# A Fourier front with a root for each of its first two tiles, even and odd sums in one PSUM bank, and two input loads on another queue

## The chip, the cores and the metric

The kernel runs on one core of a Trainium2 chip. Its time is that of one execution on the device, in microseconds (us), as the median of several runs. The engines are TensorE (PE: matmuls; PEld: its weight loads), VectorE (DVE), ScalarE (ACT) and GpSimd (POOL); SyncE (SP) issues most transfers, GpSimd the accumulating ones and a few more.

## The reference

Two sequences of 512 tokens with 1024 features pass through two layers. Layer 0 mixes by a Fourier transform, layer 1 by grouped attention, and each is followed by a squared-ReLU MLP; a last norm ends it. All data are float32. The change touches only the mixer of layer 0:

```python
def rms_norm(x, g):
    x32 = x.astype(jnp.float32)
    y = x32 * lax.rsqrt(jnp.mean(x32 * x32, axis=-1, keepdims=True) + EPS)
    return (y * g.astype(jnp.float32)).astype(x.dtype)

def fourier_mix(h, w_out):
    B, S, _ = h.shape
    hg = h.astype(jnp.float32).reshape(B, S, N_FGROUPS, F_GROUP)
    f = jnp.fft.fft2(hg, axes=(1, 3), norm="ortho").real
    f = f.reshape(B, S, D_MODEL).astype(h.dtype)
    return f @ w_out
...
    x = x + fourier_mix(rms_norm(x, fourier_norm[j]), fourier_w_out[j])
```

The real part of the transform over tokens and the 128 features of a group is a product of cosines minus a product of sines. The kernel folds both axes: sums and differences of mirrored features (`p`, plus, and `m`, minus), and even and odd parts over tokens, halve the work.

## The kernel before, in words

The front runs from the start to about 72 us, in an order written out by hand for all engines (`manual_schedule`): each engine works through its own list strictly in the order in which the program names the operations, and waits where an operand, a buffer or a bank isn't ready.

The two sequences are handled one after the other. **The first** (`q == 0`) is done "exactly", with float32 operands on TensorE, where each product is two instructions; everything later splits its operands into a high and a low float32r half and multiplies three times (`mm3`, lines 80 to 83).

*The operands of the first sequence.* Four tiles of 128 tokens come in (`begin`, line 322). `Front` (from line 365) takes two tiles each: `f0` the first two, `f1` the others. Per tile: the sum of squares (ScalarE, L124), the gain (VectorE, L379), the minus (L392) and the plus (L383). `chain` runs the six steps of a reciprocal root (L135 to L140: one on ScalarE, five on VectorE) for both tiles of a `Front` at once. `scale_both` (L409, ScalarE) scales the plus, eight Nyquist columns and the minus of one tile of `f0`; that gives the first and the second operand, `parts[0]` and `parts[1]`. `f1` scales its first tile (L403) and adds or subtracts its second (`combine`, L417 to L419, VectorE) into the third operand, `parts[2]`.

*The token transform.* Features lie in four blocks of 128 (`j`). For each block `exact_even` (L473) sums three operands times cosines in one PSUM bank and `exact_odd` (L476) three operands times sines in another; `exact_nyq` (L479) is one more row set, which ScalarE and VectorE copy into `an` (L565, L566). There are eight banks, so `transform` takes blocks 0 to 2 first, operand by operand, evacuates each with two ScalarE copies (L496, L497), runs the feature stage of block 0, then block 3 and the rest. `idle` (L545) gives TensorE 61 products without use until the data are there.

*The feature stage.* `feat_stage` makes `u` (L508, L513), `v` (L521) and a Nyquist row set `en` (L522) of each block; `split` (L86 on ScalarE, then L87 on VectorE) writes their high and low halves. `nyq_out` (L535, L536) does so for `en`.

*The output weights.* `Fold` loads two halves of a block's weights on SP (L318, L319). `minus` subtracts them on VectorE (L614) and adds them by a GpSimd transfer (L615); `odd` splits the difference (L86, L87); `even_hi` and `even_lo` split the sum (L624, L628). `FoldNyq.load` prepares the Nyquist weights, a write and three reads through DRAM on GpSimd's queue (L646, L648). `odd_outs` multiplies all four blocks into eight output banks (96 matmuls in L81 to L83), which `odd_put` evacuates on ScalarE (L689, L690). `even_outs` then does the eight even outputs one by one, 13 matmuls each, the last in L666; each needs a bank that an `odd_put` has freed. `even_put` adds them on VectorE (L695).

*The second sequence.* Its tiles are loaded on SP (L299) and prepared by `g0` and `g1` between the steps above: squares, gain, minus, an adding transfer for the plus (`plus_there`, L388, GpSimd), the root, the scaling (L403), `combine` (L431 to L434, VectorE) and the splits (L443, L448). Then `transform(1)` runs, with the same code as for the first but split operands.

What decides the order of the work is thus the written lists, the eight banks, SP's and GpSimd's queues in order, and the slots of the pools.

Of the kernel before, what the change touches and what calls it, by code (L numbers as in the profile page):

```python
# [19 lines left out]
P = 128  # L20
D = 1024
# [23 lines left out]
def trunk_kernel(ctx, tc, x_in, xt_in, y_out, tables, rope, gfour, gcol, grow, gfin,  # L45
# [319 lines left out]
    class Front:  # L365


        def __init__(self, q, c):
            self.q, self.c = q, c
            self.ss, self.r = small(2), small(2)  # L370
            self.steps = rsqrt_steps(self.r[:, :2], self.ss[:, :2], 2, 1.0 / D)
            self.xg, self.p, self.m = [None] * 2, [None] * 2, [None] * 2

# [31 lines left out]
        def scale_both(self, i):  # L405
            if i == 0:
                self.n = sm.tile([P, 2, 5, 8], F32, tag="ny", name=nm("ny"), bufs=2, padded_shape=[P, 2, 8, 8])
            for out, x in ((self.p[i], self.p[i]), (self.n[:, i], eights(self.m[i])), (self.m[i], self.m[i])):
                nc.scalar.activation(out, x, AF.Copy, scale=self.r[:, i : i + 1])  # L409
            parts.append((self.p[i], self.m[i], self.n[:, i]))  # L410

        def combine(self):
            (p1, p2), (m1, m2), r, w = self.p, self.m, self.r, 8
            stt = nc.vector.scalar_tensor_tensor
            if self.q == 0:
                n = sm.tile([P, 5, 8], F32, tag="ny", name=nm("ny"), bufs=2, padded_shape=[P, 16, 8])
                stt(n, eights(m2), r[:, 1:2], eights(m1), ALU.mult, ALU.add)  # L417
                stt(m2, m2, r[:, 1:2], m1, ALU.mult, ALU.subtract)
                stt(p1, p2, r[:, 1:2], p1, ALU.mult, ALU.add)  # L419
                parts.append((p1, m2, n))  # L420
                return
# [49 lines left out]

    def exact_even(k, j, o):
        nc.tensor.matmul(o[:, :258], parts[k][0][:, j * P : (j + 1) * P], cosX[k], start=k == 0, stop=k == 2)  # L473

    def exact_odd(k, j, v):
        nc.tensor.matmul(v[:, :256], parts[k][1][:, j * P : (j + 1) * P], sinX[k], start=k == 0, stop=k == 2)  # L476
# [15 lines left out]

    def seq_evac(q, o, v):
        if q == 0:
            t = slot([P, 514], F32)
            nc.scalar.copy(t[:, :258], o[:, :258])  # L496
            nc.scalar.copy(t[:, 258:], v[:, :256])  # L497
            return t[:, :258], t[:, 258:]
# [12 lines left out]
    def feat_stage(q, j, a, b, an, en, u=None):  # L511
        if q == 0:
            nc.tensor.matmul(u[:, :258], ftX[:, :P], a, start=False, stop=True)  # L513
# [6 lines left out]
        if q == 0:  # L520
            nc.tensor.matmul(v[:, :256], ftX[:, P:], b, start=True, stop=True)  # L521
            nc.tensor.matmul(en[0:72, :258], pickX[:, pick], a, start=j == 0, stop=j == 3)  # L522
# [10 lines left out]
    def nyq_out(q, en):  # L533
        t = slot([P, 258], F32R)[0:72]
        nc.scalar.copy(t, en[0:72, :258])  # L535
        nc.vector.tensor_sub(t[64:72], en[64:72, :258], f32(t[64:72]))  # L536
        un[q] = t
# [9 lines left out]
    def transform(q, mid=lambda: None, hook=lambda at, j: None):  # L547
        on, ov = ps(), [(ps(), ps()) for _ in range(3)]
        if q == 0:
            for k in range(2):  # L550
                for j in range(3):
                    exact_even(k, j, ov[j][0])
                exact_nyq(k, on)
                for j in range(3):
                    exact_odd(k, j, ov[j][1])
            mid()
            exact_nyq(2, on)
        else:
            seq_nyq(q, 0, on)
            for j in range(3):  # L560
                seq_part(q, j, 0, *ov[j])
            mid()
            seq_nyq(q, 1, on)
        en = ps()
        nc.scalar.copy(an[0:40], on[0:40, :258])  # L565
        nc.vector.tensor_sub(an[32:40], on[32:40, :258], f32(an[32:40]))  # L566
        ab = []
        for j in range(3):
            if q == 0:
                exact_odd(2, j, ov[j][1])  # L570
                exact_even(2, j, ov[j][0])
            else:
                seq_part(q, j, 1, *ov[j])
            ab.append(seq_evac(q, *ov[j]))
            hook("seq", j)
        us = [None] * 4
        if q == 0:
            us[0] = feat_nyq(ps(), 0, True)
        feat_stage(q, 0, *ab[0], an, en, us[0])
        hook("feat", 0)  # L580
        o3 = ps(), ps()
        if q == 0:
            for k in range(3):
                exact_even(k, 3, o3[0])
            for k in range(3):
                exact_odd(k, 3, o3[1])
        else:
            for c in range(2):
                seq_part(q, 3, c, *o3)
        ab.append(seq_evac(q, *o3))  # L590
        hook("seq", 3)
        if q == 0:
            us[1:] = [feat_nyq(ps(), j, True) for j in range(1, 4)]
        feat_stage(q, 1, *ab[1], an, en, us[1])
        hook("feat", 1)
        feat_stage(q, 2, *ab[2], an, en, us[2])
        hook("feat", 2)
        feat_stage(q, 3, *ab[3], an, en, us[3])
# [32 lines left out]
    class FoldNyq:  # L631
# [7 lines left out]
        def load(self):  # L639
# [6 lines left out]
            nc.gpsimd.dma_start(self.d.rearrange("i a (b f) -> (a b) i f", b=16), f32(h[:, :2]))  # L646
            for r, i in ((0, 0), (32, 1), (64, 0)):
# [54 lines left out]
    with tc.manual_schedule(engines={ET.PE, ET.Activation, ET.DVE, ET.Pool, ET.SP}):  # L702
# [16 lines left out]
        f1.squares(0)  # L719
        f0.minus(1)  # L720
        f0.plus(1)
        f0.scale_both(0)
        f1.gain(0)
        f1.squares(1)
        f1.chain(1, 2)
        f0.scale_both(1)
        f1.minus(0)
# [1321 lines left out]
```

## Time and profile before

| what | value |
|---|---|
| three timed runs | 1680.16, 1681.12, 1679.12 us; median 1680.16 |
| the profiled execution | 1682.5 us |
| its span, first to last instruction | 1680.5 us |
| mean granted TensorE clock | 0.998 |
| ScalarE, GpSimd busy | 873.4 us (52%), 394.5 us (23%) |
| transfers | 302.99 MB, mean 180 GB/s |

A line of a timeline reads: start, duration (both us), engine, line of the program, operation, what is written from what (with buffer numbers left out), shape and type, how many alike were merged; in brackets the time for which the engine stood still before it and what ended that. A line of a table of groups has the count, then busy time and mean ns of one, then the idle time ahead. A line of the table of waits says who waited for whom: total us, times, longest. In a row of the table of stretches each engine's busy time is followed by the number of its instructions that touch the stretch, then come the granted clock, the share of the DMA engines' time and GB/s.

### The profile page before, as it was taken

The numbers are of one execution on the slowest core, as the hardware profiler recorded it, in microseconds if no ns is written. First come the engines' busy times: TensorE is split into PE (matmuls) and PEld (weight loads), VectorE is DVE, ScalarE is ACT, GpSimd is POOL, SyncE is SP. The second block draws the span as 40 slices with busy tenths as digits, with TensorE's granted clock in tenths as the row PEclk, the third lists the DMA queues.
The fourth block names the chain that finished last, engine by engine and source line by source line (L and its number), as shares of the span: only waits on it lengthen the run. The fifth ranks groups of instructions, "written<-read, shape, count | busy, mean of one in ns | idle before, by whom it ended". The sixth has DMA issues, their size and how long they took to land.

```text
span 1680.5 us, 22279 instructions
## 1 busy us (share of the span) xinstructions
PE 1666.0 (99%) x7845; PEld 1387.7 (83%) x7845; DVE 1258.9 (75%) x1848; ACT 873.4 (52%) x1537; POOL 394.5 (23%) x364
## 2 busy tenths in 40 slices
PE   9999999999999999999999999999999999999998
PEld 8988888888888888788878888888888888888887
DVE  8879776557786779869888877777855487878865
ACT  6766444456343425447698854554544553433334
POOL 3321443221000001325544303004422220000002
PEclk9999999999999999999999999999999999999999
DMA  9843655459775757425501146334544696757532
GB/s 310 262 151 111 209 194 182 145 176 371 242 231 170 254 171 225 168 65 196 168 1 39 63 164 224 124 114 160 209 156 155 226 367 203 232 158 237 176 102 100
DMA packets 122047, 302.99 MB, mean 180 GB/s; under 512 B 12200, under 2 KB 13352, under 8 KB 121936
## 3 DMA queue, kind: packets, MB, share of 16 engines
q1 hardware_dynamic: 98576, 254.05, 43.6%
q0 software_dynamic: 8960, 21.05, 5.9%
q10 hardware_dynamic: 14400, 26.48, 4.2%
q8 instruction: 61, 1.00, 0.2%
q14 instruction: 50, 0.41, 0.1%
HBM read 218.11 MB, written 82.38 MB: 179 GB/s over the span
## 4 chain that ended last, share of the span: by engine, by line
PE 87%; DVE 6%; ACT 3%; issue 2%; DMA 2%; POOL 0%; SPq 0%; DVEq 0%; ACTq 0%; POOLq 0%
PE ps L907 69%; PE ps L83 5%; PE ps L81 5%; PE ps L82 5%; PE ps L1482 1%; DVE w L87 1%; ACT t L1474 1%; ACT u L86 1%; DVE u L87 1%; DVE u L219 1%; DVE u L235 1%; DVE u L1113 0%; DMA u<-w_four 0%; DMA u<-x 0%; PE ps L172 0%
## 5 line engine op out<-in xcount | busy, mean ns | idle before, releaser
L907 PE MATMUL ps<-u,w 128*128 128x512 f32 x4944 | 1133.3, 390 | 2.9 <-DVE w L87 2.1
L907 PEld LDWEIGHTS ps<-u,w 128*128 128x128 f32 x4944 | 927.5, 188 | 199.1 <-DVE w L87 3.2
L86 ACT CAST w<-raw 128x1024 fp32r<-128x1024 f32 (+1 forms) x216 | 214.0, 996 | 310.9 <-PE ps L907 229.0
L87 DVE TENSOR_TENSOR w<-raw,w 128x1024 fp32r<-128x1024 f32 (+1 forms) x216 | 252.3, 1172 | 77.6 <-ACT w L86 77.3
L86 ACT CAST u<-u 128x1024 fp32r<-128x1024 f32 x144 | 145.2, 1049 | 83.8 <-PE ps L907 36.5
L87 DVE TENSOR_TENSOR u<-u,u 128x1024 fp32r<-128x1024 f32 x144 | 173.3, 1230 | 19.0 <-ACT u L86 17.9
L907 PE MATMUL ps<-u,u 128*128 128x512 f32 x600 | 143.1, 389 | 0.1
L1142 POOL DMA_DIRECT2D raw<-w_sum x32 | 27.7, 866 | 469.3 <-DMA raw<-w_sum 197.9
L1113 DVE TENSOR_TENSOR u<-ps,u 128x512 f32<-128x512 f32 x160 | 109.6, 686 | 37.2 <-PE ps L907 34.4
L1023 POOL TENSOR_TENSOR u<-u 128x512 f32<-128x512 f32 x28 | 37.7, 1345 | 424.7 <-ACT u L920 424.7
L907 PEld LDWEIGHTS ps<-u,u 128*128 128x128 f32 x600 | 112.5, 188 | 23.8 <-ACT u L938 0.5
L81 PE MATMUL ps<-u,u 128*128 128x512 f32 (+2 forms) x340 | 128.8, 381 | 0.4 <-ACT t L1474 0.3
L82 PE MATMUL ps<-u,u 128*128 128x512 f32 (+2 forms) x340 | 124.2, 366 | 0.4 <-DVE u L87 0.3
L83 PE MATMUL ps<-u,u 128*128 128x512 f32 (+2 forms) x340 | 124.4, 366 | 0.1
L164 POOL TENSOR_TENSOR t<-t,t 128x512 f32<-128x512 f32 (+1 forms) x54 | 77.8, 1446 | 190.6 <-ACT t L160 189.9
L919 ACT ACTIVATE t<-t 128x512 f32<-128x512 f32 x64 | 40.5, 632 | 109.8 <-DVE t L992 99.8
L87 DVE TENSOR_TENSOR u<-ps,u 128x512 fp32r<-128x512 f32 (+3 forms) x112 | 68.5, 635 | 7.9 <-ACT u L86 7.3
L83 PEld LDWEIGHTS ps<-u,u 128*128 128x128 f32 x340 | 64.2, 189 | 10.5 <-DVE u L448 0.5
L81 PEld LDWEIGHTS ps<-u,u 128*128 128x128 f32 x340 | 64.3, 189 | 10.1 <-ACT u L86 1.5
L82 PEld LDWEIGHTS ps<-u,u 128*128 128x128 f32 x340 | 64.4, 189 | 9.2 <-DVE u L87 1.4
L979 DVE TENSOR_TENSOR t<-ps,u 128x512 f32<-128x512 f32 x32 | 22.0, 688 | 60.5 <-PE ps L907 52.7
L1476 POOL TENSOR_SCALAR t<-t,s 128x512 f32<-128x512 f32 x64 | 47.3, 740 | 74.0 <-DVE s L1475 60.1
(260 smaller groups left out, 2029.7 us busy)
## 6 DMA issues: line engine op xcount, KB each, us to landing
raw<-w_up SPq DMA_DIRECT2D x80, 512.0 KB, 4.6
u<-spill_t SPq DMA_DIRECT2D x60, 512.0 KB, 6.8
raw<-w_sum SPq DMA_DIRECT2D x56, 512.0 KB, 5.7
u<-spill_b SPq DMA_DIRECT2D x45, 512.0 KB, 6.2
spill_t<-u SPq DMA_DIRECT2D x84, 256.0 KB, 2.0
spill_b<-t ACTq DMA_DIRECT2D x60, 256.0 KB, 4.3
raw<-w_row SPq DMA_DIRECT2D x28, 512.0 KB, 5.2
park<-u SPq DMA_DIRECT2D x24, 512.0 KB, 4.5
```

The costliest lines, as they stand in the source:

```text
L81: nc.tensor.matmul(out, lh, rh, start=first, stop=False)
L82: nc.tensor.matmul(out, lh, rl, start=False, stop=False)
L83: nc.tensor.matmul(out, ll, rh, start=False, stop=last)
L86: nc.scalar.copy(dst_hi, src)
L87: eng.tensor_sub(dst_lo, src, f32(dst_hi))
L164: nc.gpsimd.tensor_add(acc[q][:, :n], acc[q][:, :n], s[:, :n])
L907: nc.tensor.matmul(o, w[x][:, sl], h[k][y], start=first and k + i == 0, stop=k == n - 1 and i == 2, skip_group_check=not first)
L919: nc.scalar.activation(t, src, AF.Relu)
L1023: eng.tensor_sub(t[:, 0], b12, b11)
L1113: nc.vector.tensor_add(x, o, x)
L1142: nc.gpsimd.dma_start(s[:, 1], w[:, 3], accum_op=ALU.add)
L1476: nc.gpsimd.tensor_scalar(p, p, sm_[:, :1], 1.0, ALU.mult, ALU.mult)
```

## The change

For the first sequence only:

- `f0` takes a root for each of its two tiles (`alone`), plus ahead of minus; `scale_both` is cut into `scale_plus` and `scale_minus`.
- `combine` for `f1` is cut into `combine_minus` and `combine_plus`; the odd part of the third operand comes first.
- Even and odd sums of a block share one bank: columns 0 to 256 and 257 to 511. `exact_open` writes zeros (the Nyquist buffer, then still zero, as moving operand) over the whole bank with `start`, and all other products add. The four blocks so take four banks, and all four go through operands 1 and 2 ahead of operand 3; of operand 3 come the odd sums, the Nyquist rows, the even sums. One ScalarE copy of 512 columns evacuates a block (`exact_evac`). The feature stages of all four follow, with 257 and 255 columns where there were 258 and 256.
- The warm-up has 46 products where it had 61.
- `fold[0].odd` and `fold[1].minus` come after the four evacuations, `fold[2].minus` after the feature stage of block 0, `fold[1].odd` after that of block 1, `fold[3].minus`, `fold[2].odd` and `fold[3].odd` after that of block 3. The reads of the Nyquist weights (`get`) come behind two weight additions on GpSimd's queue.
- The work of `g0` that stood ahead of the odd outputs' code is spread between the even weights' splits; its root's last four steps come after the third low part, and its first scaling stands ahead of all eight `odd_put` on ScalarE, of which four now come ahead of its second.
- Tiles 2 and 3 of the second sequence are loaded on GpSimd's queue, behind the last weight addition.

```diff
+        def alone(self, i, a, b):
+            if i not in self.each:
+                c = slice(i, i + 1)
+                self.each[i] = rsqrt_steps(self.r[:, c], self.ss[:, c], 1, 1.0 / D)
+            for step in self.each[i][a:b]:
+                step()
...
+    def exact_open(o):
+        nc.tensor.matmul(o, an[:, :P], filler.unsqueeze(1).broadcast_to([P, 4, P]), start=True, stop=True)
+
     def exact_even(k, j, o):
-        nc.tensor.matmul(o[:, :258], parts[k][0][:, j * P : (j + 1) * P], cosX[k], start=k == 0, stop=k == 2)
-
-    def exact_odd(k, j, v):
-        nc.tensor.matmul(v[:, :256], parts[k][1][:, j * P : (j + 1) * P], sinX[k], start=k == 0, stop=k == 2)
+        nc.tensor.matmul(o[:, :257], parts[k][0][:, j * P : (j + 1) * P], cosX[k][:, :257], start=False, stop=k == 2,
+                         skip_group_check=True)
+
+    def exact_odd(k, j, o):
+        nc.tensor.matmul(o[:, 257:], parts[k][1][:, j * P : (j + 1) * P], sinX[k][:, 1:256], start=False, stop=k == 2,
+                         skip_group_check=True)
...
+    def exact_evac(o):
+        t = slot([P, 512], F32)
+        nc.scalar.copy(t, o)
+        return t[:, :257], t[:, 257:]
...
+    def transform_exact(o, mid, hook):
+        on = ps()
+        for k in range(2):
+            for j in range(4):
+                exact_even(k, j, o[j])
+            exact_nyq(k, on)
+            for j in range(4):
+                exact_odd(k, j, o[j])
+        mid()
+        for j in range(4):
+            exact_odd(2, j, o[j])
+        exact_nyq(2, on)
+        put_an(on)
+        ab = []
+        for j in range(4):
+            exact_even(2, j, o[j])
+            ab.append(exact_evac(o[j]))
+        hook("seq", 3)
+        en = ps()
+        us = [feat_nyq(ps(), j, True) for j in range(4)]
+        for j in range(4):
+            feat_stage(0, j, *ab[j], an, en, us[j])
+            if j < 3:
+                hook("feat", j)
+        nyq_out(0, en)
+        hook("feat", 3)
...
-        idle(ps(), 61)
+        idle(ps(), 46)
+        pairs = [ps() for _ in range(4)]
+        for o in pairs:
+            exact_open(o)
         f0.squares(0)
         f0.gain(0)
+        f0.plus(0)
+        f0.alone(0, 0, 2)
+        f0.squares(1)
+        f0.alone(0, 2, 6)
         f0.minus(0)
-        f0.plus(0)
-        f0.squares(1)
+        f0.scale_plus(0)
         f0.gain(1)
-        f0.chain(0, 6)
+        f0.alone(1, 0, 2)
+        f0.scale_minus(0)
+        f0.alone(1, 2, 6)
         f1.squares(0)
...
         def hook0(at, j):
             if at == "seq":
...
+                fold[1].minus()
+                wn.get()
+                fold[0].odd()
+            elif j == 0:
+                fold[2].minus()
+            elif j == 1:
+                fold[1].odd()
             elif j == 3:
+                fold[3].minus()
+                for t in range(2, 4):
+                    load_x(1, t, nc.gpsimd)
+                fold[2].odd()
                 fold[3].odd()
...
         o = odd_outs(0, range(KC))
+        fold[0].even_hi()
+        g0.squares(0)
+        fold[0].even_lo()
+        g0.gain(0)
+        fold[1].even_hi()
+        g0.minus(0)
+        g0.plus_there(0)
+        g0.squares(1)
         g0.chain(0, 2)
-        fold[0].even_hi()
-        fold[1].even_hi()
+        fold[1].even_lo()
+        fold[2].even_hi()
+        g0.gain(1)
+        fold[3].even_hi()
+        g0.minus(1)
+        g0.plus_there(1)
+        fold[2].even_lo()
         g0.chain(2, 6)
-        fold[0].even_lo()
-        fold[1].even_lo()
+        fold[3].even_lo()
         g0.scale(slice(0, 1))
-        fold[2].even_hi()
-        fold[2].even_lo()
-        odd_put(0, 0, o[0])
-        fold[3].even_hi()
-        fold[3].even_lo()
-        for fo in range(1, 4):
+        for fo in range(4):
             odd_put(0, fo, o[fo])
         g0.scale(slice(1, 2))
```

Behind the front the instructions of every engine follow in the same order as before.

More of the change, by code (lines that the diff above doesn't have):

```diff
@@ L512, in feat_stage @@
         if q == 0:
-            nc.tensor.matmul(u[:, :258], ftX[:, :P], a, start=False, stop=True)
+            nc.tensor.matmul(u[:, :257], ftX[:, :P], a, start=False, stop=True)
         else:
@@ L545, in idle, with put_an @@
             nc.tensor.matmul(o[:, :256], filler, filler.unsqueeze(1).broadcast_to([P, 2, P]), start=True, stop=True)
[L547 to L564, printed above, removed]
+    def put_an(on):
@@ L567, in transform @@
+    def transform(q, hook):
+        on, ov = ps(), [(ps(), ps()) for _ in range(3)]
+        seq_nyq(q, 0, on)
+        for j in range(3):
+            seq_part(q, j, 0, *ov[j])
+        seq_nyq(q, 1, on)
+        en = ps()
+        put_an(on)
         ab = []
         for j in range(3):
[L569 to L573, printed above, removed]
+            seq_part(q, j, 1, *ov[j])
@@ L840, in hook1 @@
                     square(0, 7)
-        transform(1, hook=hook1)
+        transform(1, hook1)
         for fo in range(KC):
```

118 lines of the change are left out of this document (47 added, 71 removed).

## The prediction

> **What bounds the kernel now.** I read the page first (engines and chain), then TensorE's waits, then the timeline of the first 60 us, the only stretch whose instructions the change touches. The profiled execution took 1682.5 us for a span of 1680.5 us, so 2.0 us lie around the span; the median of the three timed runs is 1680.16, that is 2.3 us under the profiled one. I work against 1682.5 and shift at the end.
>
> ```profile
> span 1680.5 us, 22279 instructions
> ...
> PE 1666.0 (99%) x7845; PEld 1387.7 (83%) x7845; DVE 1258.9 (75%) x1848; ACT 873.4 (52%) x1537; POOL 394.5 (23%) x364
> ...
> PE 87%; DVE 6%; ACT 3%; issue 2%; DMA 2%; POOL 0%; SPq 0%; DVEq 0%; ACTq 0%; POOLq 0%
> ```
>
> ```profile
> PE ps L907 <- DVE w L87: 2.1, 2, 1.9
> ...
> PE ps L473 <- ACT t L409: 1.0, 1, 1.0
> ...
> PE ps L83 <- DVE w L628: 0.5, 1, 0.5
> ```
>
> TensorE is 99% busy and holds 87% of the chain that ended last. Its whole execution has few waits, and two of the three longest lie in the front: 1.0 us before the first Fourier product (L473) and 0.5 us in the first even output (L83). From there on the engine has next to no slack, so I let a shift of the front pass to the end one for one. What the change can save is a microsecond or two at the start; what it can cost is the cover under which VectorE and ScalarE prepare the next stage. So the sum is made over three in-order engines.
>
> **The start.** The rows of the first tile, before:
>
> ```profile
> 6.08 1.23 DVE L379 TENSOR_TENSOR u<-u,u 128x1024 f32<-128x1024 f32 x1 [4.97 <-DMA u<-x]
> 7.34 0.69 DVE L392 TENSOR_TENSOR t<-u 128x512 f32<-128x512 f32 x1
> ...
> 9.69 0.16 DVE L135 TENSOR_SCALAR s<-s 128x2 f32<-128x2 f32 x1
> ...
> 10.34 0.16 DVE L140 SCALAR_TENSOR_TENSOR s<-s,s 128x2 f32<-128x2 f32 x1
> ...
> 10.59 0.71 ACT L409 ACTIVATE t<-t,s 128x512 f32<-128x512 f32 x1
> ...
> 11.35 1.57 PE L473 MATMUL ps<-u,t 128*128 128x258 f32 x6 [1.03 <-ACT t L409]
> ```
>
> The root over two tiles stands behind the second tile's gain. After: gain at 6.08, plus at 7.34 (0.61 until the next), then the tile's own root, 9.69 to 10.50, 0.81 us for five steps, ends at 8.76; ScalarE follows 0.09 later, 0.71 long, and TensorE starts at 9.6: **-1.75 us**. The shortened warm-up and the four opening products have no row before. Bounds: 15 warm-up products fewer free 15 x 0.15 = 2.25 us (61 took 9.16 us), four openings of 128x512 cost nothing at best and 4 x 0.39 = 1.6 us at worst (mean of the costliest matmul group, 390 ns). The warm-up so ends before 10.0; I take no cost, and 0.4 at worst is swallowed by the wait for the third operand.
>
> **TensorE up to the feature stage.**
>
> ```profile
> 12.85 0.63 PE L479 MATMUL ps<-u,ny 128*40 128x258 f32 x2
> ...
> 13.41 1.56 PE L476 MATMUL ps<-u,t 128*128 128x256 f32 x6
> ...
> 22.96 1.47 PE L473 MATMUL ps<-u,t 128*128 128x258 f32 x6
> ...
> 24.26 1.46 PE L476 MATMUL ps<-u,t 128*128 128x256 f32 x6
> ...
> 29.64 0.47 PE L81 MATMUL ps<-u,u 128*128 128x256 f32 x1
> ```
>
> Six of these instructions take 24.26 - 22.96 = 1.30 us, 0.217 each (a product is two of them); a Nyquist pair 0.56 (12.85 to 13.41). The columns lost (258 to 257, 256 to 255) are under 0.5%: nothing. Four blocks and two operands are 2 x (16 x 0.217 + 0.56) = 8.1, with 0.1 to 0.2 at each switch 8.5: TensorE wants the third operand at 18.1. VectorE gives its odd part at about 18.5, whose last two steps now are
>
> ```profile
> 17.32 0.30 DVE L417 SCALAR_TENSOR_TENSOR ny<-t,s,t 128x40 f32<-128x40 f32 x1
> ...
> 17.66 0.75 DVE L418 SCALAR_TENSOR_TENSOR t<-t,s,t 128x512 f32<-128x512 f32 x1
> ```
>
> From 8.76 on: minus 0.61, gain 1.14, second root 0.81, plus and minus 1.22, two gains 2.28, third root 0.81, two minuses and a plus 1.83, Nyquist rows 0.3, combination 0.75. Then odd 1.73, Nyquist 0.56, even 1.73, four products with the Nyquist rows 0.7, twelve feature pairs of 0.434: the feature stage ends at 28.4 where the odd outputs now begin at 29.64. A lead of **1.2 us** is left there.
>
> **What the lead meets: VectorE.** Before, ScalarE copied block 0 and went straight on to the weight split. Now the split of `fold[0]` stands behind the copies of all four blocks. The rows for its price:
>
> ```profile
> L86 ACT CAST u<-u 128x1024 fp32r<-128x1024 f32 x4 | 4.3, 1064 | 0.0
> ...
> L181 ACT COPY t<-ps 128x512 f32<-128x512 f32 x2 | 1.2, 582 | 0.0
> ```
>
> ```profile
> 20.69 1.23 DVE L614 TENSOR_TENSOR u<-raw,u 128x1024 f32<-128x1024 f32 x1
> ...
> 21.83 1.22 DVE L87 TENSOR_TENSOR u<-u,u 128x1024 fp32r<-128x1024 f32 x1
> ...
> 28.29 2.12 DVE L87 TENSOR_TENSOR u<-ps,u 128x257 fp32r<-128x257 f32 x6
> ```
>
> Block 0 is whole at 18.5 + 1.73 + 0.56 + 0.43 + 0.15 = 21.4; four copies at 0.55 reach 23.6, the cast 24.65, and VectorE subtracts at 24.75. It has begun `fold[0].minus` at 19.7, behind the plus sums of the third operand, has `fold[1].minus` done by 22.7 and then stands still for some **2.0 us**; before, L87 followed L614 at 21.83 without a gap. From 24.75 VectorE has no more gaps, and its order is fixed: nine 1024-wide operations (six for the odd weights and the minuses left, three even low parts) at 1.14, two gains at 1.25, two minuses at 0.61, eight PSUM differences at 0.35 (L87, six in 2.12), the Nyquist difference 0.4 and the root of `g0` 0.8: 10.3 + 2.5 + 1.2 + 2.8 + 0.4 + 0.8 = 18.0. The root of `g0` is ready at **42.8**.
>
> **The wait that decides.**
>
> ```profile
> 36.96 0.16 DVE L140 SCALAR_TENSOR_TENSOR s<-s,s 128x2 f32<-128x2 f32 x1
> 37.04 2.36 DVE L628 TENSOR_TENSOR w<-raw,w 128x1024 fp32r<-128x1024 f32 x2
> ...
> 42.05 1.22 DVE L628 TENSOR_TENSOR w<-u,w 128x1024 fp32r<-128x1024 f32 x1 [1.26 <-ACT w L624]
> ```
>
> ```profile
> 37.16 0.73 ACT L403 ACTIVATE t<-t,s 128x512 f32<-128x512 f32 x1
> ...
> 39.44 0.36 ACT L689 COPY u<-ps 128x255 f32<-128x255 f32 x1
> 39.70 0.39 ACT L690 ACTIVATE u<-ps 128x255 f32<-128x255 f32 x1
> ...
> 43.51 0.76 ACT L403 ACTIVATE u<-u,s 128x512 f32<-128x512 f32 x1
> ```
>
> ```profile
> 41.34 0.28 PE L81 MATMUL ps<-u,w 128*128 128x258 f32 x1
> 41.46 0.29 PE L82 MATMUL ps<-u,w 128*128 128x258 f32 x1
> ...
> 43.33 0.39 PE L83 MATMUL ps<-u,w 128*128 128x258 f32 x1 [0.50 <-DVE w L628]
> ```
>
> Two L628 in 2.36 us of 1.22 each give the 1.14. The even outputs' matmuls start 0.12 apart (41.34, 41.46), and the odd outputs' are as long. Before, the root (36.96) came ahead of the even low parts, and ScalarE's scaling (37.16) and first evacuation (39.44) were done before TensorE asked for a bank at 41.34. After, three low parts stand ahead of the root, and on ScalarE all eight evacuations stand behind the scaling that waits for it. The odd outputs fill all eight banks, so the first even output can't begin before `odd_put(0)`: 42.8 + 0.1 + 0.62 + 0.5 = 44.0. Before it began at 41.34 and lost 0.5, in effect 41.84: **+2.2 us**, in which the lead of 1.2 is gone. The second scaling falls at 42.9 + 0.62 + 4 x 0.52 = 45.6 against 43.51, **+2.1**, and with it what prepares the second sequence. As the transfer of the last even weights bound its low part (42.05) and no longer does, I round down: both engines arrive **2.0 us** later at the second transform, where little slack is left to swallow it:
>
> ```profile
> 58.38 0.68 DVE L448 TENSOR_TENSOR u<-t,u 128x512 fp32r<-128x512 f32 x1
> ```
>
> ```profile
> 59.12 0.38 PE L83 MATMUL ps<-u,u 128*128 128x256 f32 x1
> ```
>
> TensorE's product at 59.12 follows the end of this difference (59.06) at once. Profiled 1682.5 + 2.0 = 1684.5; for the median 1680.16 + 2.0 = **1682.2 us**.
>
> **The moved loads.** Two input tiles leave SP's queue for GpSimd's, behind the four weight additions and ahead of the two additions of `g0`. Earlier bytes become later ones, so nothing is won or lost by volume. The issues on GpSimd:
>
> ```profile
> L388 POOL DMA_DIRECT2D u<-u x4: 854/866/893, 36.3 to 51.5; - x4
> ...
> DMA to landing us min/median/max: 3.3/4.4/6.0
> ```
>
> After, the second addition of `g0` can't be issued before VectorE's minus at about 41.0 and lands between 44.3 and 47.0; the combination wants it at 46.4. I take the median, no cost; up to 0.6 if late.
>
> **Rivals.**
>
> *A: the idle gap slows TensorE's clock.* The odd outputs start at 28.4, lose 0.5 to banks freed by VectorE, take 96 x 0.12 and end near 40.4; until 44.0 the engine waits 3.6 us. The kernel's own start shows what a rested engine does:
>
> ```profile
> 2.00:3.00 1.00, 1.00 (x6) 1.00 (x6) 0.00 (x0) 0.65 (x2) 0.45 (x1) 1.00 0.87 180
> ...
> 5.00:6.00 1.00, 1.00 (x11) 1.00 (x10) 0.00 (x0) 0.00 (x0) 0.00 (x0) 1.00 1.07 434
> ```
>
> Six warm-up products touch a microsecond at first, eleven after about 4 us, at a granted clock of 1.00 in both. If 3.6 us of rest bring that back, some 4 us run at about half speed, 1.7 us more: 1683.9. [...] No row before shows a gap of that length. Chance 0.15.
>
> *B: the lead survives (the other side).* If VectorE keeps pace, because ScalarE's four copies overlap the products more than I count and its 1024-wide rows run closer, so that the root of `g0` is there by 39.5, the evacuations finish before TensorE asks at 40.1: the 1.2 us stay, with the 0.5 of L83. The price is -1.7: 1678.5. For it stand the shorter start and the 1.3 us in which VectorE waited for the last weight's transfer at 42.05. Against it stand 18.0 us of fixed VectorE work behind 24.75. Chance 0.12.
>
> *C: the additions behind the moved loads come late.* If they land at 47 or more, the second sequence's operands are late by another 1 us: 1683.2. Chance 0.12. That the first root wins nothing at all, because something else starts TensorE at 11.35, changes little: VectorE decides either way, and it is inside the forecast.
>
> **How the numbers follow.** Forecast 0.61 at 1682.2 (1681.0 to 1683.4); A 0.15, B 0.12, C 0.12. 1679.0 to 1684.8 leaves out a third of B, the late half of A with C on top, and ends of the others: under 0.2. A measurement of this kernel tells about 0.2% from no change, 3.4 us: 1676.8 to 1683.5. Faster than that only B at its best, 0.04; slower two thirds of A, a third of C and the forecast's upper end, 0.24; within, 0.72.
>
> **What would show it.** Right: first L492 product at 9.6, odd outputs from about 28.4, a VectorE gap of 2 us before the first 1024-wide L87 near 24.7, the root of `g0` near 43, a TensorE wait of 3 to 4 us before the first even output, evacuated by ScalarE. Wrong: that wait missing or put down to a DMA; an even output's matmuls at twice their 0.12 us (A); the combination of `g0` waiting for a DMA (C); a shift at 58 us that isn't found at the end.

## The result and the profile after

The changed kernel takes 1684.50 us (median of 10 runs, 1682.22 to 1686.53), the kernel before 1679.47 us beside it (10 runs, 1678.22 to 1684.17): a ratio of **1.0025, 95% interval 1.0015 to 1.0034**, or some +4.2 us (the quotient of the two medians, 1.0030, lies in that interval). Forecast were +2.0, and 1681.0 to 1683.4 as the band around them; the whole range was 1679.0 to 1684.8, and 1684.50 lies at its upper end. The profiled execution after took 1684.58 us, its span 1682.7 us.

From the page of the kernel after (span, engines, chain by engine):

```profile
span 1682.7 us, 22264 instructions
...
PE 1666.0 (99%) x7834; PEld 1388.0 (82%) x7834; DVE 1259.0 (75%) x1853; ACT 873.2 (52%) x1535; POOL 393.8 (23%) x366
...
PE 85%; DVE 6%; ACT 3%; DMA 2%; issue 2%; POOL 0%; DVEq 0%; ACTq 0%; POOLq 0%; SPq 0%
```

TensorE's sum hasn't moved by 0.1 us, so the page doesn't find the loss. TensorE's waits do:

```profile
PE ps L81 <- ACT u L719: 4.0, 1, 4.0
...
PE ps L945 <- DVE w L87: 0.8, 2, 0.6
```

The first row is new: the first even output waits for the first evacuation of an odd one. VectorE, then ScalarE, on the way there:

```profile
21.30 0.42 DVE L573 TENSOR_TENSOR u<-ps,u 8x258 fp32r<-8x258 f32 x1 [0.51 <-ACT u L572]
21.75 1.23 DVE L641 TENSOR_TENSOR u<-raw,u 128x1024 f32<-128x1024 f32 x1
24.50 1.23 DVE L87 TENSOR_TENSOR u<-u,u 128x1024 fp32r<-128x1024 f32 x1 [1.52 <-ACT u L86]
...
42.99 0.16 DVE L140 SCALAR_TENSOR_TENSOR s<-s,s 128x2 f32<-128x2 f32 x1
...
46.73 0.75 DVE L449 SCALAR_TENSOR_TENSOR u<-u,s,u 128x512 f32<-128x512 f32 x1 [1.02 <-ACT u L412]
```

```profile
43.19 0.72 ACT L412 ACTIVATE t<-t,s 128x512 f32<-128x512 f32 x1 [3.42 <-DVE s L140]
43.81 0.35 ACT L718 COPY u<-ps 128x255 f32<-128x255 f32 x1
44.07 0.38 ACT L719 ACTIVATE u<-ps 128x255 f32<-128x255 f32 x1
...
45.91 0.78 ACT L412 ACTIVATE u<-u,s 128x512 f32<-128x512 f32 x1
```

The split of `fold[0]` stands behind the four copies (1.52 us of rest), the root of `g0` comes at 42.99, the scaling that ScalarE waits 3.42 us for is the first of its list, and the first bank is free at about 44.5. So far this is the chain that was forecast. The new thing is TensorE behind the wait:

```profile
9.50 1.68 PE L492 MATMUL ps<-u,t 128*128 128x257 f32 x7
...
44.50 0.58 PE L81 MATMUL ps<-u,w 128*128 128x258 f32 x1 [3.98 <-ACT u L719]
44.88 0.42 PE L82 MATMUL ps<-u,w 128*128 128x258 f32 x1
45.10 0.42 PE L83 MATMUL ps<-u,w 128*128 128x258 f32 x1
...
49.61 0.31 PE L82 MATMUL ps<-u,w 128*128 128x258 f32 x1
49.76 0.28 PE L83 MATMUL ps<-u,w 128*128 128x258 f32 x1
49.88 0.28 PE L695 MATMUL ps<-u,u 72*128 72x258 f32 x1
```

From 44.88 to 49.61 the matmuls start 0.215 us apart; at 49.76 they are back to the 0.12 of the kernel before. These are 22 intervals of 0.095 us too much, **2.1 us**. The table of stretches shows the cause as the granted clock (third number from the end of a row):

```profile
41.00:42.00 1.00, 0.00 (x0) 0.00 (x0) 1.00 (x2) 0.00 (x0) 0.02 (x1) 1.00 0.77 129
42.00:43.00 1.00, 0.00 (x0) 0.00 (x0) 0.90 (x5) 0.00 (x0) 0.86 (x1) 0.91 0.02 4
43.00:44.00 1.00, 0.00 (x0) 0.00 (x0) 1.00 (x2) 0.81 (x2) 0.76 (x1) 0.50 0.65 115
...
48.00:49.00 1.00, 1.00 (x7) 1.00 (x7) 0.84 (x3) 1.00 (x5) 0.00 (x0) 0.50 1.01 319
49.00:50.00 1.00, 1.00 (x8) 1.00 (x7) 0.47 (x1) 0.97 (x2) 0.74 (x1) 0.68 1.18 385
50.00:51.00 1.00, 1.00 (x11) 1.00 (x10) 1.00 (x2) 1.00 (x2) 0.16 (x1) 1.00 0.60 141
```

A mean of 0.91 between 1.00 and 0.50 puts the fall at 42.82, in the middle of the rest; 0.68 puts the return at 49.64. The page's row of 40 slices doesn't show 6.8 us, and the means of the two profiled executions (0.997 against 0.998) hardly do, since the kernel before has a slow phase of its own in that execution (at 697.7 us, shown further down). Over many runs the mean does tell: the kernel after stands at 0.996 to 0.998 in all ten, the kernel before, as run beside the experiments, at 0.999 in 80 of 102. Single values say little: the last microseconds of both profiled executions stand at 0.50 too (1677.3 to 1680.5 before, 1677.8 to 1682.7 after), so that without such a phase the mean would be an estimated 0.999; the two counts together point to a fall in most executions of the kernel after.

To compare executions I count from the first gain on VectorE, since the first tile lands at another time in each (that gain starts between 5.67 and 6.94 us). Each column is the start of an instruction in the timeline of the profiled execution, less that gain's start: the first Fourier product, the first odd output, the last step of `g0`'s root, the first even output, the second transform's first matmul (shape 128*40), and the first L172 product, with which the front ends. The ratio is against the kernel before on the same chip.

| kernel | product | odd | root | even(0) | 2nd transform | front ends | ratio (95%) |
|---|---|---|---|---|---|---|---|
| before | 5.27 | 23.56 | 30.88 | 35.26 | 48.60 | 65.87 | 1 |
| after | 3.72 | 22.29 | 37.21 | 38.72 | 53.58 | 70.19 | 1.0025 (1.0015 to 1.0034) |
| keep_busy | 3.47 | 22.29 | 37.22 | 38.73 | 51.35 | 68.74 | 1.0018 (1.0010 to 1.0026) |
| evac_first | 3.49 | 22.31 | 37.25 | 34.61 | 51.45 | 68.06 | 1.0017 (1.0008 to 1.0025) |
| split_early | 3.48 | 22.30 | 36.25 | 37.76 | 53.07 | 69.68 | 1.0020 (1.0011 to 1.0029) |
| loads_back | 3.49 | 22.29 | 37.24 | 38.75 | 53.91 | 70.54 | 1.0026 (1.0016 to 1.0036) |
| root_alone | 3.48 | 24.12 | 31.44 | 35.81 | 48.31 | 65.08 | 1.0007 (0.9998 to 1.0015) |
| root_before_low | 3.70 | 22.29 | 34.33 | 35.85 | 50.43 | 67.04 | 1.0011 (1.0003 to 1.0020) |
| split_evac_first | 3.56 | 22.30 | 36.25 | 33.99 | 48.96 | 65.60 | 0.9999 (0.9991 to 1.0008) |
| split_evac_gpsimd | 3.93 | 22.29 | 36.04 | 34.30 | 48.77 | 65.38 | 0.9999 (0.9990 to 1.0007) |
| low_first | 3.48 | 22.29 | 38.77 | 34.00 | 47.85 | 71.31 | 1.0020 (1.0011 to 1.0029) |
| before_low_first | 5.25 | 23.54 | 40.92 | 36.16 | 49.97 | 71.07 | 1.0032 (1.0020 to 1.0045) |
| low_between | 3.48 | 22.31 | 37.40 | 34.00 | 46.49 | 68.71 | 1.0024 (1.0015 to 1.0033) |
| odd_sums_first | 3.48 | 22.28 | 37.38 | 33.98 | 48.37 | 69.06 | 1.0024 (1.0015 to 1.0033) |

The front of the kernel after ends 4.32 us later, and the whole is 4.2 us longer: the shift passes to the end. Per row the two agree within some 2 us, so the landmarks say where time goes and the ratios how much of it is certain.

### The profile page after: what moved, and what is told of

The parts are those of the page before. It is cut to its first block, busy times and chain, and to the rows that moved or that the text cites. A ratio compares the mean times of both kernels' runs of the same rounds, so it can differ in the third digit from the quotient of the medians.

```text
span 1682.7 us, 22264 instructions
## 1 busy us (share of the span) xinstructions
PE 1666.0 (99%) x7834; PEld 1388.0 (82%) x7834; DVE 1259.0 (75%) x1853; ACT 873.2 (52%) x1535; POOL 393.8 (23%) x366
## 4 chain that ended last, share of the span: by engine, by line
PE 85%; DVE 6%; ACT 3%; DMA 2%; issue 2%; POOL 0%; DVEq 0%; ACTq 0%; POOLq 0%; SPq 0%
PE ps L945 67%; PE ps L81 5%; PE ps L82 5%; PE ps L83 5%; DMA raw<-w_sum 1%; PE ps L1520 1%; ACT u L86 1%; ACT t L1512 1%; DVE w L87 1%; DVE u L87 1%; DVE u L219 1%; DMA u<-w_qkv 1%; DVE u L1151 1%; DVE u L235 1%; PE ps L172 0%
## 5 line engine op out<-in xcount | busy, mean ns | idle before, releaser
L87 DVE TENSOR_TENSOR u<-ps,u 128x512 fp32r<-128x512 f32 (+3 forms) x112 | 68.5, 635 | 8.0 <-ACT u L86 7.5
```

The lines of the kernel that those rows point to most:

```text
L87: eng.tensor_sub(dst_lo, src, f32(dst_hi))
```

## The experiments

The theory after the result: the loss is the late first bank (the forecast's chain) and the slow clock that the rest brings on (rival A on top). Rivals: the moved loads, the new form of the transform itself, or VectorE's list alone. Line numbers are those of each kernel.

**keep_busy** fills the rest: TensorE does the last odd output twice more, 24 matmuls that write the same sums again.

```diff
         o = odd_outs(0, range(KC))
+        for _ in range(2):
+            for k in range(4):
+                u, fs = uv[0, k][:, :, 256:512], slice(7 * P, 8 * P)
+                mm3(o[7], wo[k][0][:, fs], wo[k][1][:, fs], u[:, 0], u[:, 1], k == 0, k == 3)
```

> The changed kernel, but TensorE sums the last odd output two more times after the first (24 matmuls, 2.9 us, the same numbers again); the wait for the bank stays, only its rest is filled. Theory: the rest before the first even output shrinks from 4.0 to about 1.1 us while that output begins at the same 44.5; its matmuls are 0.12 us apart instead of 0.215, so the clock's share is measured by itself: 22 matmuls x 0.095 = 2.1 us less than the changed kernel, ratio to the kernel before about 1.0012. Rival (VectorE bounds the stretch from 50 to 60 us anyway, so a slow clock costs nothing): time as of the changed kernel, ratio 1.0025, even with matmuls 0.12 apart. Rival (the half speed has another cause than the rest, such as the evacuations or transfers at that place): matmuls still 0.215 apart.

The even output starts as late as in the kernel after (38.73), after a rest of 1.1 us, and its matmuls are 0.122 apart, so the half speed came from the rest. In the stretches:

```profile
45.00:46.00 1.00, 0.33 (x2) 0.33 (x3) 1.00 (x2) 1.00 (x5) 1.00 (x3) 1.00 1.02 176
46.00:47.00 1.00, 1.00 (x11) 1.00 (x10) 0.89 (x3) 1.00 (x5) 1.00 (x3) 1.00 0.35 25
```

Eleven matmuls in a microsecond at a clock of 1.00. The second transform starts 2.23 us earlier than in the kernel after, the price of the clock; 0.8 of it goes again before the front ends, where TensorE now waits 0.3 us for VectorE's last split. What is left at the end of the front, +2.87 us, is the price of the late bank without the clock. The ratio alone doesn't settle this: 1.0018 (1.0012 was expected) is not told from 1.0025, so the split into 2.87 and 1.45 rests on the landmarks of one execution each. The mean clock agrees: 0.999 in seven of twelve runs, never reached by the kernel after.

**evac_first** puts ScalarE's first four evacuations ahead of the scaling that waits for the root.

```diff
-        g0.scale(slice(0, 1))
         for fo in range(4):
             odd_put(0, fo, o[fo])
+        g0.scale(slice(0, 1))
         g0.scale(slice(1, 2))
```

> The changed kernel with the first four evacuations of the odd outputs moved ahead of the first scaling of g0 on ScalarE; nothing else differs. Theory (the evacuations stand behind a scaling that waits for VectorE's late root, TensorE so rests 4.0 us and comes back at half speed): the first even output begins near 40.5 us; TensorE then waits in it for the second, third and fourth low part in pieces of at most 2 us, until VectorE has written the fourth near 44.3; matmuls stay 0.12 us apart. The even outputs end near 57 instead of 59.3, and the kernel takes about 3 to 4 us less than the changed one: ratio to the kernel before 1.0000 to 1.0008. Rival (VectorE's list is late whatever ScalarE does, the wait on ScalarE only shows it): no more than 1 us is won, ratio 1.0020 or above. Rival (moved loads): ratio as of the changed kernel, 1.0025.

The even output starts 4.11 us earlier and the front ends only 2.13 earlier. Two waits for the low parts take the place of the one removed, and the stretches show what they do:

```profile
PE ps L83 <- DVE w L655: 2.1, 2, 1.2
```

```profile
44.00:45.00 1.00, 0.04 (x1) 0.00 (x0) 1.00 (x2) 0.94 (x2) 0.89 (x1) 1.00 0.80 141
45.00:46.00 1.00, 0.78 (x5) 0.78 (x6) 1.00 (x2) 1.00 (x4) 1.00 (x4) 0.95 0.71 121
46.00:47.00 1.00, 1.00 (x7) 1.00 (x6) 1.00 (x4) 0.81 (x4) 1.00 (x3) 0.50 0.48 53
```

Two rests of 0.97 and 1.18 us, 0.6 us of matmuls between them, are followed by the half clock as well, from 45.9 to 49.3. The expectation had the matmuls 0.12 us apart and a ratio of at most 1.0008; the wait for the bank was the cause of the late start, as it said, but the clock takes part of the gain.

**split_early** takes `fold[0].odd` and `fold[1].minus` behind the first of the four copies.

```diff
             ab.append(exact_evac(o[j]))
-        hook("seq", 3)
+            hook("seq", j)
...
```

> The changed kernel with the second weight subtraction and the first odd weight split put behind the first block's evacuation instead of the fourth's. Theory: VectorE's gap of 1.5 us before its first 1024-wide split closes, all that follows on it up to the root of g0 comes 1.0 to 1.5 us earlier (root near 41.8 instead of 43.1), TensorE's rest falls to 2.5 to 3 us. If a rest of that length doesn't bring the slow clock back, the kernel takes 3 to 3.5 us less than the changed one (ratio 1.0004 to 1.0008); if it does, 1.0 to 1.5 us less (ratio about 1.0017). Rival (evacuations of the other blocks now come late and TensorE loses what VectorE wins): the feature stage ends 0.5 us or more later and the time stays at 1.0025.

VectorE's rest falls from 1.52 to 0.5 us, and the root comes 0.96 us earlier. The wait shrinks only by 0.37 to 3.6, since the odd outputs, without their wait of 0.35 us for a bank, end 0.6 earlier too, and the half clock stays (0.216 apart). The forecast's gap was a real term, worth 1 us at the root and 0.5 at the end of the front.

**loads_back** puts the two moved loads back on SP's queue.

```diff
-        for t in range(2):
+        for t in range(NT):
             load_x(1, t)
...
-                for t in range(2, 4):
-                    load_x(1, t, nc.gpsimd)
```

> The changed kernel with the two input tiles of the second sequence back on SP's queue. Theory: nothing that decides hangs on them; ratio to the kernel before as of the changed kernel, 1.0025, within 0.0005, and the root of g0 still near 43. Rival C (the additions behind the moved loads come late): about 1 us less, and the combination of g0 earlier by that.

Every landmark is that of the kernel after to 0.35 us. The moved loads cost nothing, as the combination's wait for ScalarE instead of a transfer (46.73 above) already said.

**root_alone** gives the kernel before the root per tile, plus ahead of minus, and 54 warm-up products; its transform is as it was.

```diff
-        idle(ps(), 61)
+        idle(ps(), 54)
         f0.squares(0)
         f0.gain(0)
-        f0.minus(0)
         f0.plus(0)
+        f0.alone(0, 0, 2)
         f0.squares(1)
+        f0.alone(0, 2, 6)
...
```

> The kernel before with one part of the change alone: a root for each of the two first tiles, plus ahead of minus, 54 fillers. Theory (the early start is real but nothing behind it uses it, because the third operand and then VectorE's fixed work set the pace): first product 3.5 to 3.7 us after the first gain instead of 5.3, odd outputs within 0.3 us of 23.6, root of g0 within 0.3 us of 30.9, ratio 1.0000 (0.9995 to 1.0005). Rival (the early start is worth its length): odd outputs at 21.8, ratio 0.9990. Rival (the rest that opens in front of the third operand slows TensorE): a clock of 0.5 behind it and a ratio over 1.0005.

The first product comes 1.79 us earlier and the odd outputs 0.56 later: what is won at the start is spent in one wait for the third operand.

```profile
PE ps L491 <- DVE ny L429: 1.8, 1, 1.8
```

The expectation had the odd outputs and the root within 0.3 us of the kernel before; both come some 0.55 late, and the front ends 0.79 earlier all the same, which stays unexplained. Behind that wait the products keep their pace (pairs start 0.43 us apart, at 20.40, 20.83 and 21.26, or 0.217 an instruction as in the kernel before), so the last rival falls. The early start by itself buys nothing that the ratio shows (1.0007, not told from 1). So the lead of 1.27 us in the kernel after comes with the changed transform; that it has more to do ahead of that operand is my reading, not tried by itself.

**root_before_low** has `g0`'s gains and root ahead of the four low parts. (What this and later expectations call odd sums are `g0`'s minus and plus.)

```diff
-        fold[0].even_lo()
         g0.gain(0)
...
         g0.chain(0, 2)
-        fold[1].even_lo()
+        g0.gain(1)
         fold[2].even_hi()
-        g0.gain(1)
-        fold[3].even_hi()
         g0.minus(1)
         g0.plus_there(1)
-        fold[2].even_lo()
         g0.chain(2, 6)
-        fold[3].even_lo()
+        fold[3].even_hi()
+        for j in range(4):
+            fold[j].even_lo()
```

> The kernel after, with g0's gains, odd sums and root ahead of all four low parts on VectorE; the scaling still ahead of the first evacuations. Theory (VectorE's whole list up to the last low part bounds the first even output, whichever piece of it stands last): root at about 33.8 us after the first gain instead of 37.2, even(0) starts at 35 to 35.7 instead of 38.7, but waits for low parts inside it until about 38.5; the rests are over 1 us each and close together as in the run with the evacuations first, so 3.4 us at half clock are likely; second transform at 51 to 51.8, front end at 67.5 to 68.5, ratio 1.0010 to 1.0018. Rival (only the root's lateness costs): second transform at 49, front end at 66 and ratio 1.0000 to 1.0003.

Root 2.9 us and even output 2.9 us earlier, and the waits are small and apart:

```profile
PE ps L81 <- ACT u L719: 1.1, 1, 1.1
PE ps L83 <- DMA u<-dcos: 0.5, 1, 0.5
PE ps L83 <- DVE w L655: 0.5, 1, 0.5
```

The clock stays at 1.00 (in every stretch from 32 to 55 us), against my expectation, and the front ends 3.15 us earlier than in the kernel after, between the theory (67.5 to 68.5) and the rival (66).

**split_evac_first** joins split_early and evac_first.

> Both single repairs at once: the first fold's split behind the first evacuation and the odd evacuations ahead of both scalings. Theory (rest and clock are what is lost): the last low part comes about 1.0 us earlier than with the evacuations first alone (37.6 instead of 38.6 after the first gain), the rests inside even(0) sum to about 1.1 us instead of 2.15, the clock stays at 1.00; second transform at 48.8 to 49.5, front end at 66 to 66.8, ratio 1.0000 to 1.0006. Rival (the two repairs don't add, the clock falls all the same): second transform at 50.4 or later and ratio 1.0010 or more.

Together they bring more than the sum of the two (0.51 and 2.13 us): the front ends 4.6 us earlier than in the kernel after, 0.3 earlier than before, and the ratio is 0.9999. With the changed transform in place and only two orders changed the loss is gone, so the form of the transform is not its cause. The rests inside the first even output still sum to 1.9 us (1.1 were expected), and the clock did not fall in the front of this execution (1.00 in every stretch from 32 to 55 and from 56 to 68 us). Its eleven runs have mean clocks of 0.999 (six), 0.998 (four) and 0.997 (one), so it may fall in some of them.

**split_evac_gpsimd** adds one edit to it.

```diff
-            nc.vector.tensor_sub(self.b, self.a, self.b)
+            (nc.gpsimd if self.j > 1 else nc.vector).tensor_sub(self.b, self.a, self.b)
```

> As the one above, and the subtractions of the third and fourth fold on GpSimd instead of VectorE. Theory (VectorE's list up to the last low part is the bound): 2 x 1.15 us leave VectorE, so the last low part comes at about 35.3 to 36.3 us after the first gain, even(0) starts at 34.6 and waits under 0.5 us in all, clock 1.00, second transform at 47.9 to 48.5, front end at 65.0 to 66.0, ratio 0.9993 to 1.0000: level with the kernel before or ahead of it. Rival (GpSimd's subtraction of 128x1024, estimated at 3.0 us from twice the 1.5 us of a 128x512 one, makes the transfers and odd splits behind it late): VectorE waits for the folds, second transform as in the run above or later, ratio 1.0003 or more.

The ratio is as expected, but not by the expected way: the root comes only 0.2 us earlier, though 2.3 us of work have left VectorE. GpSimd, then VectorE:

```profile
25.28 2.67 POOL L641 TENSOR_TENSOR u<-raw,u 128x1024 f32<-128x1024 f32 x1
...
28.97 2.71 POOL L641 TENSOR_TENSOR u<-u,u 128x1024 f32<-128x1024 f32 x1
```

```profile
26.67 2.37 DVE L87 TENSOR_TENSOR u<-u,u 128x1024 fp32r<-128x1024 f32 x1 [0.52 <-ACT u L86]
28.96 1.41 DVE L87 TENSOR_TENSOR u<-ps,u 128x257 fp32r<-128x257 f32 x4
...
30.85 3.17 DVE L87 TENSOR_TENSOR u<-u,u 128x1024 fp32r<-128x1024 f32 x2
```

VectorE's difference of two SBUF operands takes 2.37 us instead of 1.22: GpSimd's ends at 27.95, and 1.1 later VectorE's ends. The differences with a PSUM operand beside the second subtraction are as long as ever (four in 1.41). VectorE so ends about its own length behind GpSimd, as if it had worked after it and not beside it; why, no run here shows.

**low_first** and **before_low_first** put the low parts ahead of `g0`'s gains, after both repairs in the one, in the kernel before (with the evacuations ahead of the scalings) in the other, where `g0`'s squares, gains and sums also leave the transform for the place behind the odd outputs. The diff of the first:

```diff
         fold[0].even_hi()
         g0.squares(0)
         fold[0].even_lo()
-        g0.gain(0)
         fold[1].even_hi()
-        g0.minus(0)
-        g0.plus_there(0)
+        fold[1].even_lo()
         g0.squares(1)
...
+        g0.gain(0)
+        g0.minus(0)
+        g0.plus_there(0)
         g0.chain(0, 2)
...
```

> The kernel after with three things moved: the first fold's split behind the first evacuation, the odd evacuations ahead of both scalings, and all four low parts ahead of g0's gains, odd sums and root. Theory (the last low part on VectorE is what holds up TensorE, and nothing needs g0's root until the second transform): the last low part ends at about 34 to 35 us after the first gain instead of 37.5, even(0) starts at 34.0 and waits under 0.5 us, clock 1.00 throughout; the root comes at 38.5 to 39.5 and is not late for the second transform, which starts at 46.3 to 47; front end at 63.8 to 64.8, ratio 0.9984 to 0.9993, the lead of 1.27 us at the odd outputs kept. Rival (the root is late for the second transform, VectorE is the bound whatever the order): second transform at 48.3 to 49, front end at 65.5 or later, ratio 0.9998 or more.

> The kernel before with its transform and its start as they were, and the order behind the odd outputs that the run above has: low parts first, then g0's gains and root, odd evacuations ahead of the scalings. Theory: odd outputs at 23.6 after the first gain, even(0) at 35.1 to 35.4 without its waits of 0.5 us, second transform at 47.6 to 48.2, front end at 64.8 to 65.5, ratio 0.9993 to 0.9999; so the run above is ahead of it by the lead of about 1.27 us, which is what the changed transform would then be worth. Rival (the order alone does it): both at the same front end and ratio.

In low_first the rests inside even(0) are gone, as the theory had it, and the front ends 5.7 us later than without this edit. The premise that nothing needs `g0` before the second transform was wrong: four evacuations stand behind its scalings on ScalarE, its plus comes by a transfer for which VectorE waits 1.96 us, and `g1` stands behind all that. The second transform then starts with its operands missing:

```profile
PE ps L81 <- ACT ny L86: 1.3, 1, 1.3
PE ps L81 <- ACT u L725: 1.2, 2, 0.6
PE ps L81 <- ACT u L719: 1.0, 1, 1.0
```

and the clock falls there, from 63.9 to 67.3. The kernel before under the same order ends its front at 71.07, and its clock falls too, at 60.3: with that order the changed transform is worth nothing that these runs show, as the rival had it.

**low_between** and **odd_sums_first** are two middle ways on top of split_evac_first: the last three low parts between `g0`'s two gains; and both gains first, the root last. The diff of low_between:

```diff
         g0.gain(0)
...
-        g0.chain(0, 2)
         fold[1].even_lo()
         fold[2].even_hi()
-        g0.gain(1)
+        fold[2].even_lo()
         fold[3].even_hi()
+        fold[3].even_lo()
+        g0.chain(0, 2)
+        g0.gain(1)
         g0.minus(1)
...
```

> As the run with the early split and the evacuations first, with the last three low parts between g0's first and second gain on VectorE. Theory (the last low part must come before TensorE is through the odd outputs, and g0's root may be about 1 us later but not 3): last low part at about 35 us after the first gain instead of 37.5, root at 37.4 instead of 36.3, no rest over 0.5 us inside even(0), clock 1.00; second transform at 47.0 to 47.8, front end at 63.8 to 64.8, ratio 0.9985 to 0.9996. Rival (1 us is too late too, because the DMA that adds the odd sums is issued 2 us later and the combination waits for it): combination at 46 or later with a wait for the DMA, scalings and evacuations behind it late, front end at 66 or later, ratio over 1.0002.

> The same, but both gains and odd sums of g0 stand behind the first low part and the other three low parts behind them, the root last. Theory: last low part at about 36.4 us after the first gain, root at 37.2, the DMA that adds the odd sums not later than in the run with the early split and the evacuations first; the rests inside even(0) sum to about 1 us; second transform at 47.8 to 48.5, front end at 64.5 to 65.3, ratio 0.9990 to 0.9999. Rival (the front is bound by VectorE's list up to the second transform and not by the low parts): front end at 65.4 to 66, ratio 0.9998 to 1.0003.

In both the theory falls. In low_between the second transform starts at 46.49, the earliest of all and 2.1 us ahead of the kernel before, and the front ends 2.8 us behind it, with the same waits as in low_first (1.0 for `ny`, 1.2 for L725) and the half clock inside the second transform:

```profile
58.00:60.00 2.00, 1.14 (x8) 0.66 (x6) 1.45 (x3) 0.34 (x3) 1.08 (x2) 1.00 0.94 167
60.00:62.00 2.00, 1.79 (x9) 1.73 (x10) 1.86 (x5) 1.52 (x5) 0.00 (x0) 0.51 1.07 207
```

In odd_sums_first the wait for `ny` is 1.8 us and the clock falls at about 61. No version here beats the kernel before; the two at 0.9999 are level with it.

## Why the prediction was right or wrong

The chain that was forecast is there, but 1684.50 lies above its own band of 1681.0 to 1683.4. The wider range held it, and by little, because it left room for a part of rival A, so it held by something that the forecast did not count on; with the late bank alone, at its measured price, the forecast would have been 1683.0 (1680.16 + 2.87). On a time over 1683.5, clear of no change, the prediction had set 0.24.

- *The start, and the lead.* First product 1.55 us earlier from the gain (1.75 said), odd outputs 1.27 (1.2 said). Right.
- *VectorE's gap.* 0.51 and 1.52 us, 2.0 together, as said, and split_early gave 1 us of it back at the root. Right.
- *18.0 us of fixed work.* From 24.50 to the start of the root's last step at 42.99 it took 18.5, of which 0.45 is one more gap. From the first gain the root is 0.5 us later than said.
- *The scaling ahead of all evacuations.* Right as a mechanism: evac_first alone moves the even output by 4.11 us. That output came at 44.50 in the kernel after (44.0 said; 0.8 later from the first gain), the second scaling at 45.91 (45.6 said; 0.6 later).
- *+2.0 us at the second transform.* The mis-sized term. Without the clock it is +2.87 at the end of the front (keep_busy); of the 0.9 too little, 0.5 is the root and the rest lies between root and bank, and I rounded down where I should not have.
- *The clock (A).* The step that failed. It costs 2.1 us of matmuls and 1.45 at the end of the front (after against keep_busy); 2.87 + 1.45 = 4.32. I gave it 0.15, since no row of before shows a rest of 3.6 us. I also had some 4 us at half speed; it was 6.8. But the trace of before shows the half clock behind a shorter rest, its longest: a wait of 1.9 us (for L907, at 694.5), 1.2 us behind whose end the clock falls, at 697.7:

```profile
694.00:696.00 2.00, 0.55 (x3) 0.13 (x1) 1.97 (x3) 0.00 (x0) 0.00 (x0) 1.00 0.78 229
696.00:698.00 2.00, 1.54 (x6) 1.29 (x7) 1.97 (x4) 0.18 (x1) 0.00 (x0) 0.92 1.03 336
698.00:700.00 2.00, 2.00 (x6) 1.51 (x6) 1.00 (x2) 2.00 (x4) 1.40 (x2) 0.50 0.89 274
700.00:702.00 2.00, 2.00 (x8) 1.60 (x7) 0.69 (x1) 0.02 (x1) 1.92 (x2) 0.73 0.89 283
```

  Six matmuls in 2 us at 0.50 where ten or eleven are usual. These rows would have made A a far likelier rival, if not the forecast: 1683.9, or 1684.7 with the late bank at its measured price. The start's row in the prediction, six matmuls in a microsecond at 1.00, is not a sign to the contrary: behind the rest seven go with 0.50 (48 to 49 us above), so that 1.00 isn't to be relied on.
- *B and C.* B is refuted by the root at 42.99, C by loads_back.
- *A reading of the waits.* The 0.5 us in the first even output is not the third longest wait of TensorE: 1.2 us before the first warm-up product and 0.7 at 1046.6 us are longer. No term hangs on it.

Two terms stay unsettled: what bounds split_evac_first at 65.6 us (VectorE's list up to `g1`'s last split is my reading, and only the failures of the last four runs speak for it), and in how many of its executions the clock falls in the front, which the mean clocks don't say.

## What to carry to other kernels

A rest of TensorE can cost twice, the wait and then matmuls at half speed (4.0 and 2.1 us here); so look at the granted clock in narrow stretches behind every wait of TensorE over a microsecond (0.97 and 1.18 us in close succession were enough in evac_first), in the trace that is already there. An early start is worth what the latest of its later operands leaves of it (1.8 us won and spent in one wait here). When work on an in-order engine is reordered, follow each moved piece to its last reader: here the orders that put all four low parts ahead of `g0`'s root left the second transform waiting for its operands or banks (0.6 to 1.8 us in one wait).

## What the runs showed of the hardware

- *The slow phases lasted 3.4 or 6.8 us.* From half-microsecond stretches, worked out as above: 6.8 us in the kernel after (42.82 to 49.64), in split_early (43.67 to 50.49) and in loads_back (44.58 to 51.40), 3.4 in evac_first (45.89 to 49.31) and low_first (63.89 to 67.30).
- *The length of a rest doesn't decide alone.* Single rests of 1.91 us (before, at 694.5) and of 1.9 (split_early, at 699) were followed by the half clock, from 697.7 and 702.4, as were the two of evac_first; but 1.1 (keep_busy), 1.9 in two pieces (split_evac_first), 1.81 (root_alone, at 16.6) and 2.59 (root_before_low, at 1550.4) were not. The last:

```profile
1550.00:1552.00 2.00, 0.42 (x2) 0.00 (x0) 1.97 (x3) 0.75 (x1) 0.00 (x0) 1.00 1.05 407
1552.00:1554.00 2.00, 0.99 (x4) 0.86 (x5) 2.00 (x3) 2.00 (x3) 0.00 (x0) 1.00 1.05 399
1554.00:1556.00 2.00, 2.00 (x10) 1.63 (x9) 2.00 (x4) 0.20 (x1) 0.00 (x0) 1.00 1.02 376
```

  What decides besides the length, no run here shows.
- *It makes part of the scatter.* The wait of 1.9 us at about 700 us is in the profiled executions of before and of split_early, and both are over the median of their kernel (1682.5 against 1679.47, 1688.84 against 1685.35). In the kernel after it was 0.6 and the clock stayed up. 1.3 us more of wait, and 3.4 us at half clock (1.7 us of work), come to an estimated 3.0. That is enough for the two profiled executions first compared to differ by only 2.1 us where the medians differ by 5.0. How often the wait comes in other executions isn't on record.
